# Three 256-column accumulations of a decoder layer's projections turned into 512-column ones with two halves

## The chip, the cores and the metric

One NeuronCore of a Trainium2 chip runs the whole layer. The metric is the device time of one execution in microseconds; lower is better. TensorE is called PE, VectorE DVE, ScalarE ACT, GpSimd POOL and SyncE SP, as in the profile.

## The reference, cut to what matters

A decoder layer of 256 tokens and width 1024: a SwiGLU half-step, a mixer with two groups of attention heads, cross-attention, a second SwiGLU half-step, and a final norm. The three projections of this case are the ones that add into the residual stream `x`:

```python
x = x + 0.5 * swiglu(rms_norm(x, g_ffn1), w_ffn1_gu, w_ffn1_down)   # down projection, 2816 -> 1024
h = rms_norm(x, g_mix)                                              # then h @ w_in, attention
...
x = x + concatenate([ya, yb]) @ w_out                               # output projection of the mixer
x = x + cross_attn(rms_norm(x, g_cross), rms_norm(mem, g_mem))      # ends with o @ w_co
x = x + 0.5 * swiglu(rms_norm(x, g_ffn2), w_ffn2_gu, w_ffn2_down)
```

Each of the three is followed by an RMS norm of the new `x` and a further projection of it (`w_in`, `w_cq`, `w_ffn2_gu`).

## The kernel before

**Number form.** A float32 operand is split into a high and a low part, and a product is high x high + low x high + high x low. Activations lie transposed, width on the partitions: a *slot* holds two contraction steps, each as 256 columns of the high part and 256 of the low part. Weights are loaded in tiles of 128 x 1024 (`raw`, four buffers), split by ACT (L125, high part) and DVE (L126, low part) into `w` (eight buffers), and the load of a tile goes out on SP's queue when its `raw` buffer is free again.

**Two ways to do one block.** A block is 128 of the 1024 output columns for all 256 tokens, accumulated in one PSUM bank. The first way (`mm2`, `mmT_run`) streams both halves of the slot in one matmul of 512 columns (L224) and the low weights against the high activations in one of 256 (L228): the bank ends with two halves that have to be added. The second way (`mm3`, L188 to L190) makes three matmuls of 256 columns into the same 256 columns of the bank.

**What follows a block.** `add_halves` adds the bank to the residual tile X0 to X7 (one per block). With 512 columns ACT copies the second half to `hv` (L301), DVE adds the first half to X (L302), then `hv` to X (L303). With 256 columns DVE does it in one instruction (L298). Then `block` makes the next projection's operand: ACT scales X into the high part of a slot (L323), DVE makes the low part (L324), ACT squares X into `sq` (L350), and POOL adds `sq` to the running sum `ssq` (L355). `hv` and `sq` share three buffers. When all eight are in, two statistics matmuls (L367, each of them two instructions for PE) sum `ssq` over the partitions; DVE (L328) and POOL (L330) make the norm's factor from it.

**The three places.** `downT` (L442) makes the down projection: two chunks of four blocks, 22 contraction steps; block 7 (the last of chunk 1) is done the second way. `addT` (L466) makes `w_out` and `w_co` with 8 steps; with `whole=c` the last block of chunk 1 is done the second way there too. For `w_co` the first chunk has an order of its own: the four blocks run side by side and end in the last round, one after the other. The next projection takes its steps in the order of X0 to X7, all four blocks abreast, so that X7 is needed last.

**What sets the order.** PE works in the order in which the program is written (`manual_schedule` for PE); small pieces of work that are put off by `later` come in when a running estimate of PE's time (`tick`) has passed their due time. The order on DVE, ACT, POOL and SP is set by the scheduler when the kernel is built, and each of these engines then works strictly in that order.

Of the kernel before, what the change touches and what calls it, by code (L numbers as in the profile page):

```python
# [21 lines left out]
FK = FF // P  # L22
# [6 lines left out]
def layer_kernel(ctx, tc, x_in, mem_in, g_ffn1, w_gu1, w_dn1, g_mix, w_in, rel_bias, g_out_a, g_out_b,  # L29
# [13 lines left out]
    def bank():  # L43
        return psp.tile([P, 512], F32, tag="bank", name="bank")
# [86 lines left out]
    def colchunk(wd, c0, n, nkt=KT):  # L131

        per = 1024 // n
        res = []
        for k0 in range(0, nkt, per):
            nk = min(per, nkt - k0)
            w = wload((lambda raw, nk=nk: raw[:, :nk * n].rearrange("p (a n) -> p a n", n=n),
                       cols(wd, k0, nk, c0, n), nk * n))
            res += [(w, i * n) for i in range(nk)]
        return res  # L140
# [36 lines left out]
    def tick(us):  # L177
        clock[0] += us
        pump()
# [7 lines left out]
    def mm3(ps, ah, al, bh, bl, start, stop):  # L187
        nc.tensor.matmul(ps, ah, bh, start=start, stop=False)  # L188
        nc.tensor.matmul(ps, al, bh, start=False, stop=False)  # L189
        nc.tensor.matmul(ps, ah, bl, start=False, stop=stop)  # L190
        tick(0.33 if ps.shape[-1] <= 256 else 0.65)

    def act(slots, k):

        s = slots[k // 2]
        o = (k % 2) * 512
        return s[:, o:o + 256], s[:, o + 256:o + 512]

    def both(slots, k):

        return slots[k // 2][:, (k % 2) * 512:(k % 2) * 512 + 512]

    def mm2(ps, wh, wl, xhl, start, stop):

        nc.tensor.matmul(ps, wh, xhl, start=start, stop=False)
        nc.tensor.matmul(ps[:, :256], wl, xhl[:, :256], start=False, stop=stop)
        tick(0.33)

    def mmT(ps, wk, xs, k, blk, start, stop):

        w, o = wk[k]
        o += blk * P
        if ps.shape[-1] == 512:
            mm2(ps, w[:, 0, o:o + P], w[:, 1, o:o + P], both(xs, k), start, stop)
        else:
            h, l = act(xs, k)
            mm3(ps, w[:, 0, o:o + P], w[:, 1, o:o + P], h, l, start, stop)

    def mmT_run(todo, wk, xs, first, last):


        for ps, k, blk in todo:
            w, o = wk[k]
            nc.tensor.matmul(ps, w[:, 0, o + blk * P:o + (blk + 1) * P], both(xs, k), start=k == first, stop=False)  # L224
            tick(0.23)
        for ps, k, blk in todo:
            w, o = wk[k]
            nc.tensor.matmul(ps[:, :256], w[:, 1, o + blk * P:o + (blk + 1) * P], both(xs, k)[:, :256],  # L228
                             start=False, stop=k == last)
            tick(0.12)  # L230

    def mmT_wide(pieces, wk, xs, k, start, stop):

        w, o = wk[k]
        h, l = act(xs, k)
        for i, (wp_, a) in enumerate(((0, h), (0, l), (1, h))):
            for blk, ps in enumerate(pieces):
                nc.tensor.matmul(ps, w[:, wp_, o + blk * P:o + (blk + 1) * P], a,  # L238
                                 start=start and i == 0, stop=stop and i == 2)
                tick(0.11)  # L240

    def projT(wk, xs, nblk, spread=False, whole=0, abreast=False):

        res = [bank() for _ in range(nblk)] if spread or abreast else []
        if spread and whole:
            res = [b[:, :256] for b in res]
            for k in range(KT):
                mmT_wide(res, wk, xs, k, k == 0, k == KT - 1)
            return res
        if spread:  # L250
            for k in range(KT):
                mmT_run([(res[blk], k, blk) for blk in range(nblk)], wk, xs, 0, KT - 1)
            return res
        if abreast:
            for b0 in range(0, nblk, 2):
                for k in range(0, KT, 2):
                    for blk in (b0, b0 + 1):
                        mmT_run([(res[blk], k, blk), (res[blk], k + 1, blk)], wk, xs, 0, KT - 1)
            return res
        return each(wk, xs, nblk, whole)  # L260

    def each(wk, xs, nblk, whole):
        for blk in range(nblk):
            b = bank()
            if blk >= nblk - whole:
                b = b[:, :256]
                for k in range(KT):
                    mmT(b, wk, xs, k, blk, k == 0, k == KT - 1)
            else:
                for k in range(0, KT, 2):  # L270
                    mmT_run([(b, k, blk), (b, k + 1, blk)], wk, xs, 0, KT - 1)
            yield b
# [23 lines left out]
    def add_halves(x, ps, scale):  # L296
        if ps.shape[-1] == 256:
            nc.vector.scalar_tensor_tensor(x, ps, scale, x, OP.mult, OP.add)  # L298
            return
        t = work.tile([P, 256], F32, tag="sq", name="hv", bufs=3)  # L300
        nc.scalar.activation(t, ps[:, 256:], AF.Copy, scale=scale)  # L301
        nc.vector.scalar_tensor_tensor(x, ps[:, :256], scale, x, OP.mult, OP.add)  # L302
        nc.vector.tensor_tensor(x, x, t, OP.add)  # L303
# [138 lines left out]
    def downT(w_dn, hid, block):  # L442

        for c in range(2):
            wk = colchunk(w_dn, c * 512, 512, FK)
            b = [bank() for _ in range(4)]
            if c == 1:
                b[3] = b[3][:, :256]

            def step(k, blk):  # L450
                if b[blk].shape[-1] == 512:
                    mmT_run([(b[blk], k, blk), (b[blk], k + 1, blk)], wk, hid, 0, FK - 1)
                else:
                    for i in (k, k + 1):
                        mmT(b[blk], wk, hid, i, blk, i == 0, i == FK - 1)

            for k in range(0, FK - 6, 2):
                for blk in range(4):
                    step(k, blk)
            for blk in range(4):  # L460
                for k in range(FK - 6, FK, 2):
                    step(k, blk)
                add_halves(X[c * 4 + blk], b[blk], 0.5)
                block(c * 4 + blk)

    def addT(wd, src, block, order=None):  # L466

        for c in range(2):
            wk = colchunk(wd, c * 512, 512)
            if c == 0 and order:  # L470
                b = [bank() for _ in range(4)]
                for step in order:
                    if callable(step):
                        step()
                        continue
                    k, blks = step
                    for blk in blks:
                        mmT_run([(b[blk], k, blk), (b[blk], k + 1, blk)], wk, src, 0, KT - 1)
                        if k == KT - 2:
                            add_halves(X[blk], b[blk], 1.0)  # L480
                            block(blk)
                continue
            for blk, ps in enumerate(projT(wk, src, 4, whole=c, abreast=(c == 0))):
                x = X[c * 4 + blk]
                add_halves(x, ps, 1.0)
                block(c * 4 + blk)
# [335 lines left out]
    with tc.manual_schedule(engines={mybir.EngineType.PE}):  # L822
        hid = gate_up(w_gu1, xs, st, (None, bias_table), (pg0, pu0))
        xs, st, block = next_x("mix")
        downT(w_dn1, hid, block)
        st.done()

# [4 lines left out]
        def head_pair(kt, op):  # L832
# [5 lines left out]
            elif kt == 7:  # L838
# [11 lines left out]
        until(lambda: len(ot) == 4)  # L850
        xs, st, block = next_x("cross")
        addT(w_out, ot, block)
        st.done(rows=False)
        PT = cross_qp(xs, K, st)
# [3 lines left out]
        xs, st, block = next_x("ffn2")  # L858
        every = range(4)
        addT(w_co, OT, block, ((0, every), (2, (0, 1)), lambda: cross_o(V, PT, OT, 2), (2, (2, 3)),  # L860
                               lambda: cross_o(V, PT, OT, 3), (4, every), (6, every)))
        st.done()

        hid = gate_up(w_gu2, xs, st, scale=0.5)
# [3 lines left out]
        ps = [[bank() for _ in HALVES] for _ in range(2)]  # L868
# [7 lines left out]
        def step(k, tb, w, p, c0, n):  # L876
            h, l = act(hid, k)
            t = slice(tb * P, tb * P + P)
            mm3(p, h[:, t], l[:, t], w[:, 0, c0:c0 + n], w[:, 1, c0:c0 + n], False, k == FK - 1)
# [78 lines left out]
```

## Time and profile before

| | us |
|---|---|
| median of 3 runs | 605.53 (605.5 to 606.17) |
| profiled execution | 605.74 |
| its span | 604.0 |
| PE busy | 595.4 |
| PE weight loads busy | 519.3 |
| DVE busy | 428.5 |
| ACT busy | 347.7 |
| POOL busy | 51.8 |

The profiled execution's time is 1.7 us above its span, which begins with the first and ends with the last instruction of the program. Busy times of PE overlap in the view, since a matmul's end is modelled; the distance from the start of one matmul to the start of the next tells what it costs. The mean granted clock of PE is 0.998 of full speed. On DVE and ACT as well the start of the next instruction can lie before the end of the last by some 0.1 us.

### The profile page before, as it was taken

How to read it: one execution, taken by the hardware profiler on the slowest of the kernel's cores; microseconds unless marked ns; L12 is line 12 of the kernel's file. 1: busy time of each engine (PE TensorE's matmuls, PEld its weight loads, DVE VectorE, ACT ScalarE, POOL GpSimd, SP SyncE). 2: the span in 40 equal slices, each digit the busy share in tenths (PEclk: the TensorE clock that was granted, in tenths of full speed). 3: DMA queues.
4: the chain of work that ended last, by engine and by line, in shares of the span. 5: the costliest groups of instructions: out<-in, count | busy, mean ns of one | idle time of the engine just before them, and what ended most of it. 6: DMA issues, size and time to landing. Idle time of an engine off the chain costs nothing.

```text
span 604.0 us, 9469 instructions
## 1 busy us (share of the span) xinstructions
PE 595.4 (99%) x3516; PEld 519.3 (86%) x3516; DVE 428.5 (71%) x716; ACT 347.7 (58%) x604; POOL 51.8 (9%) x83
## 2 busy tenths in 40 slices
PE   9999999999999999999999999999999999999995
PEld 8988888888899888888888899888888888888884
DVE  4788766887565876766897787869877877874412
ACT  6756446655554677656675565657755656653302
POOL 0000110000010102113300120003100000000000
PEclk9999999999999999999999999999999999999999
DMA  7867998677467636454446645444565565565401
GB/s 237 282 206 229 211 246 252 196 227 245 171 221 231 210 106 210 142 173 140 141 121 218 195 143 162 140 140 130 158 230 181 169 217 171 189 231 196 152 0 69
DMA packets 58989, 110.02 MB, mean 182 GB/s; under 512 B 3760, under 2 KB 14608, under 8 KB 58944
## 3 DMA queue, kind: packets, MB, share of 16 engines
q1 hardware_dynamic: 57664, 105.49, 54.1%
q0 software_dynamic: 832, 2.88, 2.8%
q10 hardware_dynamic: 448, 1.05, 0.5%
q8 instruction: 27, 0.44, 0.3%
q14 instruction: 18, 0.15, 0.1%
HBM read 107.58 MB, written 1.84 MB: 181 GB/s over the span
## 4 chain that ended last, share of the span: by engine, by line
PE 96%; issue 1%; DVE 1%; ACT 1%; POOL 0%; POOLq 0%; ACTq 0%
PE bank L224 43%; PE bank L228 22%; PE bank L188 7%; PE bank L189 7%; PE bank L190 7%; PE bank L238 5%; PE bank L518 1%; PE bank L575 1%; PE bank L558 1%; DVE w L126 0%; PE bank L770 0%; PE bank L382 0%; PE bank L779 0%; PE bank L873 0%; PE bank L604 0%
## 5 line engine op out<-in xcount | busy, mean ns | idle before, releaser
L224 PE MATMUL bank<-slot,w 128*128 128x512 f32 x1130 | 353.4, 396 | 0.0
L126 DVE TENSOR_TENSOR w<-raw,w 128x1024 fp32r<-128x1024 f32 (+1 forms) x197 | 237.3, 1219 | 84.5 <-ACT w L125 83.7
L125 ACT ACTIVATE w<-raw 128x1024 fp32r<-128x1024 f32 (+1 forms) x197 | 202.4, 1051 | 86.3 <-PE bank L190 43.4
L228 PEld LDWEIGHTS bank<-slot,w 128*128 128x128 f32 x1130 | 209.8, 188 | 48.7 <-issue 1.0
L228 PE MATMUL bank<-slot,w 128*128 128x256 f32 x1130 | 222.5, 279 | 0.0
L224 PEld LDWEIGHTS bank<-slot,w 128*128 128x128 f32 x1130 | 173.8, 189 | 2.5 <-issue 0.6
L188 PE MATMUL bank<-w,slot 128*128 128x512 f32 x152 | 60.0, 395 | 0.0
L190 PE MATMUL bank<-w,slot 128*128 128x512 f32 x152 | 59.3, 390 | 0.0
L189 PE MATMUL bank<-w,slot 128*128 128x512 f32 x152 | 59.2, 390 | 0.0
L277 ACT ACTIVATE hv<-bank 128x256 f32<-128x256 f32 x108 | 39.8, 375 | 33.7 <-PE bank L228 33.0
L320 ACT ACTIVATE slot<-u 128x512 fp32r<-128x512 f32 x22 | 13.8, 628 | 36.0 <-DVE u L434 36.0
L190 PEld LDWEIGHTS bank<-w,slot 128*128 128x128 f32 x152 | 28.5, 188 | 6.1
L188 PEld LDWEIGHTS bank<-w,slot 128*128 128x128 f32 x152 | 28.5, 188 | 6.0 <-issue 0.3
L189 PEld LDWEIGHTS bank<-w,slot 128*128 128x128 f32 x152 | 28.6, 188 | 5.5
L238 PE MATMUL bank<-slot,w 128*128 128x256 f32 x240 | 31.8, 290 | 0.0
L238 PEld LDWEIGHTS bank<-slot,w 128*128 128x128 f32 x240 | 30.1, 195 | 0.5 <-DVE slot L324 0.2
L355 POOL TENSOR_TENSOR ssq<-ssq,sq 128x256 f32<-128x256 f32 x22 | 20.5, 933 | 78.5 <-ACT sq L350 78.4
L429 ACT ACTIVATE g<-g 128x512 f32<-128x512 f32 x22 | 13.8, 631 | 20.1 <-DVE g L292 20.1
L324 DVE SCALAR_TENSOR_TENSOR slot<-X,gT,slot 128x256 fp32r<-128x256 f32 x30 | 19.4, 659 | 6.9 <-ACT slot L323 6.9
L321 DVE TENSOR_TENSOR slot<-u,slot 128x512 fp32r<-128x512 f32 x22 | 15.2, 691 | 10.7 <-ACT slot L320 10.5
L278 DVE TENSOR_TENSOR g<-bank,hv 128x256 f32<-128x256 f32 x40 | 16.5, 420 | 8.5 <-ACT hv L277 8.5
L323 ACT ACTIVATE slot<-X,gT 128x256 fp32r<-128x256 f32 x30 | 14.8, 506 | 13.0 <-DVE X L303 13.0
(128 smaller groups left out, 488.4 us busy)
## 6 DMA issues: line engine op xcount, KB each, us to landing
raw<-in_w_ffn_gu_dram SPq DMA_DIRECT2D x88, 512.0 KB, 4.6
raw<-in_w_ffn_down_dram SPq DMA_DIRECT2D x44, 512.0 KB, 4.3
raw<-in_w_ckv_dram SPq DMA_DIRECT2D x16, 512.0 KB, 5.5
raw<-in_w_in_dram SPq DMA_DIRECT2D x12, 512.0 KB, 3.7
raw<-in_w_in_dram SPq DMA_DIRECT2D x24, 256.0 KB, 4.0
raw<-in_w_out_dram SPq DMA_DIRECT2D x8, 512.0 KB, 4.5
raw<-in_w_cq_dram SPq DMA_DIRECT2D x8, 512.0 KB, 4.8
raw<-in_w_co_dram SPq DMA_DIRECT2D x8, 512.0 KB, 3.7
```

What stands on the lines that cost most here:

```text
L125: nc.scalar.activation(w[:, 0, a:b], raw[:, a:b], AF.Copy)
L126: nc.vector.tensor_tensor(w[:, 1, a:b], raw[:, a:b], w[:, 0, a:b].bitcast(F32), OP.subtract)
L188: nc.tensor.matmul(ps, ah, bh, start=start, stop=False)
L189: nc.tensor.matmul(ps, al, bh, start=False, stop=False)
L190: nc.tensor.matmul(ps, ah, bl, start=False, stop=stop)
L224: nc.tensor.matmul(ps, w[:, 0, o + blk * P:o + (blk + 1) * P], both(xs, k), start=k == first, stop=False)
L228: nc.tensor.matmul(ps[:, :256], w[:, 1, o + blk * P:o + (blk + 1) * P], both(xs, k)[:, :256], start=False, stop=k == last)
L238: nc.tensor.matmul(ps, w[:, wp_, o + blk * P:o + (blk + 1) * P], a, start=start and i == 0, stop=stop and i == 2)
L277: nc.scalar.activation(t, ps[:, 256:], AF.Copy)
L278: nc.vector.tensor_tensor(out, ps[:, :256], t, OP.add)
L324: nc.vector.scalar_tensor_tensor(l, src, g, h.bitcast(F32), OP.mult, OP.subtract)
L355: (eng or nc.gpsimd).tensor_tensor(new, self.ss, sq, OP.add)
```

## The change

The special case of the last block goes: in `downT` block 7 is accumulated in 512 columns by `mmT_run` like the other seven, and in `addT` the argument `whole=c` goes, with the same effect for block 7 of `w_out` and of `w_co`. Since `add_halves` looks at the width, these three blocks now take its three-instruction path.

```diff
         for c in range(2):
             wk = colchunk(w_dn, c * 512, 512, FK)
             b = [bank() for _ in range(4)]
-            if c == 1:
-                b[3] = b[3][:, :256]
 
             def step(k, blk):
-                if b[blk].shape[-1] == 512:
-                    mmT_run([(b[blk], k, blk), (b[blk], k + 1, blk)], wk, hid, 0, FK - 1)
-                else:
-                    for i in (k, k + 1):
-                        mmT(b[blk], wk, hid, i, blk, i == 0, i == FK - 1)
+                mmT_run([(b[blk], k, blk), (b[blk], k + 1, blk)], wk, hid, 0, FK - 1)
...
-            for blk, ps in enumerate(projT(wk, src, 4, whole=c, abreast=(c == 0))):
+            for blk, ps in enumerate(projT(wk, src, 4, abreast=(c == 0))):
                 x = X[c * 4 + blk]
                 add_halves(x, ps, 1.0)
                 block(c * 4 + blk)
```

PE's order is otherwise the same: 38 contraction steps have two matmuls instead of three, and everything else stands in its old order, the statistics matmuls too. POOL's and SP's orders are the same. On DVE and ACT the order changes at the three places only. The largest rearrangement is at the end of `w_co`. There `w_4674` to `w_4689` of the kernel before are the tiles of the first "up" chunk of the second SwiGLU, `w_4809`, `w_4814`, ... those of its next "gate" chunk; in the changed kernel the same tiles are called `w_4645` to `w_4660` and `w_4780`, `w_4785`, ... `slot_4273` (before) and `slot_4249` (now) hold X6 and X7.

DVE at the end of `w_co`, before, from the addition of X6 on:

```order
L302 SCALAR_TENSOR_TENSOR X6_94<-bank_4514,X6_94 128x256
L324 SCALAR_TENSOR_TENSOR slot_4273<-X7_95,gT_81,slot_4273 128x256
L303 TENSOR_TENSOR X6_94<-X6_94,hv_4531 128x256
L126 TENSOR_TENSOR w_4684<-raw_4682,w_4684 128x1024
L126 TENSOR_TENSOR w_4689<-raw_4687,w_4689 128x1024
L324 SCALAR_TENSOR_TENSOR slot_4273<-X6_94,gT_81,slot_4273 128x256
L126 TENSOR_TENSOR w_4809<-raw_4807,w_4809 128x1024
L126 TENSOR_TENSOR w_4814<-raw_4812,w_4814 128x1024
L328 TENSOR_SCALAR ms_4654<-bank_4651 128x2
```

DVE at the same place now:

```order
L126 TENSOR_TENSOR w_4660<-raw_4658,w_4660 128x1024
L303 TENSOR_TENSOR X6_94<-X6_94,hv_4507 128x256
L126 TENSOR_TENSOR w_4780<-raw_4778,w_4780 128x1024
L126 TENSOR_TENSOR w_4785<-raw_4783,w_4785 128x1024
L324 SCALAR_TENSOR_TENSOR slot_4249<-X6_94,gT_81,slot_4249 128x256
L302 SCALAR_TENSOR_TENSOR X7_95<-bank_4517,X7_95 128x256
L303 TENSOR_TENSOR X7_95<-X7_95,hv_4534 128x256
L126 TENSOR_TENSOR w_4790<-raw_4788,w_4790 128x1024
L324 SCALAR_TENSOR_TENSOR slot_4249<-X7_95,gT_81,slot_4249 128x256
L328 TENSOR_SCALAR ms_4625<-bank_4622 128x2
```

X7's addition and slot, which stood ahead of X6's, stand behind them now, and the splits of `w_4780` and `w_4785` (`w_4809` and `w_4814` before) have moved ahead of X6's slot.

ACT at the end of `w_co`, before, from the scaling of X5 on:

```order
L323 ACTIVATE slot_4272<-X5_93,gT_81 128x256
L350 ACTIVATE sq_4510<-X5_93 128x256
L301 ACTIVATE hv_4531<-bank_4514 128x256
L323 ACTIVATE slot_4273<-X7_95,gT_81 128x256
L125 ACTIVATE w_4689<-raw_4687 128x1024
L125 ACTIVATE w_4809<-raw_4807 128x1024
L323 ACTIVATE slot_4273<-X6_94,gT_81 128x256
L350 ACTIVATE sq_4537<-X6_94 128x256
L350 ACTIVATE sq_4569<-X7_95 128x256
L125 ACTIVATE w_4814<-raw_4812 128x1024
```

ACT at the same place now:

```order
L323 ACTIVATE slot_4248<-X5_93,gT_81 128x256
L350 ACTIVATE sq_4486<-X5_93 128x256
L301 ACTIVATE hv_4507<-bank_4490 128x256
L125 ACTIVATE w_4780<-raw_4778 128x1024
L125 ACTIVATE w_4785<-raw_4783 128x1024
L323 ACTIVATE slot_4249<-X6_94,gT_81 128x256
L350 ACTIVATE sq_4513<-X6_94 128x256
L301 ACTIVATE hv_4534<-bank_4517 128x256
L125 ACTIVATE w_4790<-raw_4788 128x1024
L323 ACTIVATE slot_4249<-X7_95,gT_81 128x256
L350 ACTIVATE sq_4540<-X7_95 128x256
```

The split of `w_4785` stands ahead of X6's scaling now (before, its counterpart `w_4814` stood behind X7's square), and X7's copy, scaling and square come after X6's.

## Rows read from the trace of the kernel before

**Rows 1.** The page: busy time of the engines; the chain by engine.
```profile
PE 595.4 (99%) x3516; PEld 519.3 (86%) x3516; DVE 428.5 (71%) x716; ACT 347.7 (58%) x604; POOL 51.8 (9%) x83
...
PE 96%; issue 1%; DVE 1%; ACT 1%; POOL 0%; POOLq 0%; ACTq 0%
```

**Rows 2.** Timeline of PE, down projection: start, us, engine, line, operation, out<-in, shapes, count.
```profile
184.03 0.28 PE L188 MATMUL bank<-slot,w 128*128 128x256 f32 x1
...
184.74 0.63 PE L224 MATMUL bank<-slot,w 128*128 128x512 f32 x2
```

**Rows 3.** Timeline of PE: begin of block 6, block 7 and what follows, `w_co`.
```profile
406.30 0.63 PE L224 MATMUL bank<-slot,w 128*128 128x512 f32 x2
...
409.09 0.28 PE L188 MATMUL bank<-slot,w 128*128 128x256 f32 x1
...
411.97 1.09 PE L224 MATMUL bank<-slot,w 128*128 128x512 f32 x4
```

**Rows 4.** Timeline of PE: steps of X6 and X7 in the projection behind `w_co`.
```profile
420.50 1.21 PE L224 MATMUL bank<-slot,w 128*128 128x512 f32 x4
421.55 0.40 PE L228 MATMUL bank<-slot,w 128*128 128x256 f32 x2
421.79 0.50 PE L367 MATMUL bank<-ones,ssq 128*128 128x2 f32 x4
...
422.47 1.08 PE L224 MATMUL bank<-slot,w 128*128 128x512 f32 x4
```

**Rows 5.** Timeline of ACT behind `w_co`; in brackets the idle time before and its releaser.
```profile
414.97 0.37 ACT L301 ACTIVATE hv<-bank 128x256 f32<-128x256 f32 x1
415.23 0.50 ACT L323 ACTIVATE slot<-X,gT 128x256 fp32r<-128x256 f32 x1
415.63 1.99 ACT L125 ACTIVATE w<-raw 128x1024 fp32r<-128x1024 f32 x2
...
419.03 1.07 ACT L125 ACTIVATE w<-raw 128x1024 fp32r<-128x1024 f32 x1 [0.39 <-DMA raw<-in_w_ffn_gu_dram]
```

**Rows 6.** Timeline of DVE behind `w_co`.
```profile
413.13 0.41 DVE L302 SCALAR_TENSOR_TENSOR X<-bank,X 128x256 f32<-128x256 f32 x1
413.46 0.41 DVE L298 SCALAR_TENSOR_TENSOR X<-bank,X 128x256 f32<-128x256 f32 x1
...
416.48 0.47 DVE L324 SCALAR_TENSOR_TENSOR slot<-X,gT,slot 128x256 fp32r<-128x256 f32 x1
416.88 0.41 DVE L303 TENSOR_TENSOR X<-X,hv 128x256 f32<-128x256 f32 x1
417.21 2.35 DVE L126 TENSOR_TENSOR w<-raw,w 128x1024 fp32r<-128x1024 f32 x2
419.48 0.96 DVE L324 SCALAR_TENSOR_TENSOR slot<-X,gT,slot 128x256 fp32r<-128x256 f32 x1
420.36 2.89 DVE L126 TENSOR_TENSOR w<-raw,w 128x1024 fp32r<-128x1024 f32 x2
```

**Rows 7.** Timeline of POOL behind `w_co`.
```profile
415.20 0.74 POOL L355 TENSOR_TENSOR ssq<-ssq,sq 128x256 f32<-128x256 f32 x1 [2.28 <-ACT sq L350]
418.47 2.56 POOL L355 TENSOR_TENSOR ssq<-ssq,sq 128x256 f32<-128x256 f32 x2 [2.53 <-ACT sq L350]
```

**Rows 8.** Instructions that write or read the tile raw, 403 to 425 us.
```profile
DMA to landing us min/median/max: 3.5/3.6/3.6
```

**Rows 9.** Timeline of PE and DVE behind the down projection and behind `w_out`.
```profile
199.30 0.96 DVE L324 SCALAR_TENSOR_TENSOR slot<-X,gT,slot 128x256 fp32r<-128x256 f32 x1
...
205.54 0.50 PE L367 MATMUL bank<-ones,ssq 128*128 128x2 f32 x4
...
206.22 1.08 PE L224 MATMUL bank<-slot,w 128*128 128x512 f32 x4
...
354.18 1.21 DVE L126 TENSOR_TENSOR w<-raw,w 128x1024 fp32r<-128x1024 f32 x1
...
362.46 0.50 PE L367 MATMUL bank<-ones,ssq 128*128 128x2 f32 x4
```

**Rows 10.** Busy time by stretch: us, PE, PEld, DVE, ACT, POOL, PEclk, DMA, GB/s.
```profile
380.00:390.00 10.00, 9.36 (x66) 8.43 (x65) 9.25 (x18) 7.25 (x15) 0.00 (x0) 1.00 0.59 167
```

## The prediction

> **What bounds the kernel now.** I read the page first: TensorE (PE) is busy for 595.4 of 604.0 us and 96% of the chain that ended last is PE's [rows 1]. So two things count: how long PE's own stream is, and where PE has to wait. The change shortens the stream a little and lengthens, at three places, what VectorE (DVE) and ScalarE (ACT) do after the last block. I therefore went to PE's timeline at the three places for the price of a block, and then to the places where PE first needs what the last block leaves behind. There are two such needs: the slot of X7 (the eighth contraction step of the next projection), and the sum of squares, which the statistics matmuls (L367) read. The statistics matmuls stand in the middle of the seventh step at the third place: two of four L228, then L367 at 421.79, then the other two [rows 4]. PE works in its written order, so whoever makes L367 late makes everything behind it late.
>
> **What PE saves.** A pair of contraction steps was six matmuls of 256 columns; it becomes two of 512 and two of 256, the same 1536 columns. In w_co's last-but-one block (that form already) four pairs take 409.09 - 406.30 = 2.79 us; the last block takes 411.97 - 409.09 = 2.88 [rows 3]. So 0.09 us at each output projection. In the down projection a pair of the old form takes 0.71 us [rows 2] against 2.79 / 4 = 0.70; over 11 pairs that is 0.1 to 0.25, and I take 0.2. Together 0.3 to 0.45, taken as 0.4 us, all of it on the path. [...]
>
> **What is added.** Each last block had one DVE instruction (L298, 0.41 us) from PSUM into X. Now it has an ACT copy of the second half (L301, 0.37 [rows 5]), a DVE multiply-add (L302) and a DVE add (L303), each 0.41 like L298 [rows 6]. Three times 1.2 us on engines with room: by busy time it costs nothing. It costs where PE is waiting at the end of the chain. So I go through the places.
>
> **First place, the down projection.** The next projection needs X7's slot after seven of its eight steps, at 206.22, and the statistics at 205.54 [rows 9]. X7's slot was ready at 199.30 + 0.96 = 200.3. Two short instructions and the two or three weight splits that the new order puts ahead of it (1.14 us each, from 417.21 to 419.48 for two [rows 6]) make it some 203. Covered by about 3 us: nothing.
>
> **Second place, w_out.** Here the ACT queue decides. The new order has X6, then a copy for X7, then two weight splits, then X7. The second of these needs a load that is issued only when an earlier split has freed its buffer. In the old order a split at 354.18 frees one [rows 9]; in the new one the split moves up by the two instructions that no longer stand ahead of it, 0.66 us, to 353.52, and ends at 354.7. A load lands 3.6 us after issue [rows 8], 358.4; ACT's split takes 1.07 [rows 5], then X7's scaling and square 0.8: 360.2. POOL adds the square by 361.1 if free, 361.9 if DVE holds it up as in [rows 7]. L367 starts at 362.46 [rows 9]. That is 0.5 us or more of cover: nothing, but little.
>
> **Third place, w_co.** Here there is no cover. The order of w_co ends its first four blocks together, so ACT and DVE are behind: block 6 leaves PE at 409.09, but its copy runs at 414.97 [rows 3, 5]. PE already waited a little for X6's slot in the kernel before: ready at 419.48 + 0.96 = 420.44, and PE's step starts at 420.50 [rows 4, 6]. X7 was ahead of X6 then, since its short form jumped the queue (L298 at 413.46, slot at 416.48). In the changed order X7 comes last, and more weight splits stand before X6. I walk the new DVE order with the start-to-start times of [rows 6] (0.33 for L302, L303; 1.14 for a split; 0.88 for L324 with POOL beside it, 0.40 alone):
> X5's L302 at 413.13, unchanged; split 413.46; X5's L303 414.60; split 414.93; X5's slot 416.07; X6's L302 416.95; split 417.28; X6's L303 418.41; two splits 418.74 and 419.88; X6's slot at 421.0, ready at 421.5 to 422.0; X7's L302 421.4 to 421.9, its L303 done 422.1 to 422.6. The second of those two splits follows ACT's, and ACT's waits for a load issued at the end of the split of 413.46, at 414.7: landed 418.3, split by 419.4. So DVE is the later of the two, and the load, in front of X6 in ACT's queue, is hidden by 0.5 us.
> Then ACT: X7's scaling 0.40 and square 0.40 to 423.0 or 423.5. POOL's add takes 0.1 to start and 0.74 [rows 7], up to 1.0 with a split beside it: 423.9 to 424.6. PE's L367 follows 0.1 us behind, at 424.0 to 424.7 instead of 421.79. **Lost: 2.2 to 2.9 us**; I take 2.5, since POOL and DVE do overlap in this walk. In it lies the earlier wait for X6's slot, 421.5 or later instead of 420.50. X7's slot, after one more split, comes at 423.7 to 424.6 and is needed 0.68 us behind L367 (422.47 - 421.79), so it adds nothing.
> The spread between the ends comes from POOL and DVE: L324 takes 0.47 alone (416.48) and 0.96 while POOL adds (419.48), and POOL's two adds took 2.56 instead of 1.48 [rows 6, 7]. [...]
>
> **Sum.** The 0.3 us gained at the first two places moves the start of this chain forward with PE; the 0.09 of the third block doesn't, as PE waits anyway. 2.5 - 0.3 = 2.2 us (1.9 to 2.6). Behind this stretch PE's stream is gapless and gives nothing back. Against the profiled execution, 605.74: 607.9. The median of the runs, 605.53, lies 0.2 below it: **607.7 to 607.8**. What a measurement can tell from no change is about 0.2%, 1.2 us: above 606.7 counts as slower.
>
> **Rivals.** (a) *Not slower.* The last block's chain stays under PE's work at the third place as at the other two, and only the gain is left: 605.5 - 0.4 = 605.1. It decides at two points: X6's slot ready by 420.4 and the squares summed by 421.7. For it speaks that the other two places have 3 and 0.5 us of cover by the same rows; against it that the walk misses these points by 1.1 and 2.2 us, and that X6's slot was already late. It would need two of the splits to be out of the way. Chance 0.13. (b) *A second hole, at w_out.* If the load behind ACT's split takes 1 us longer, or POOL is held up twice, L367 at 362.46 slips by up to 0.7, on top of the forecast: 608.3 to 608.6. Chance 0.07. (c) *The clock falls in the new holes.* Two waits of about 1 us each within 4 us are new. Were the granted clock halved for the next 2.5 to 5 us of work, that work would take twice as long: 610.3 to 612.8. Against it: around 384 PE had about 0.6 us without work and the granted clock stayed 1.00 [rows 10]. Chance 0.03. (d) *Faster by over 1.2 us*: the saved PE time has 0.45 us at most, and no row shows a wait that the change takes away. Chance 0.01. That the change does nothing is excluded: PE's order has 38 matmuls fewer.
>
> **How the numbers follow.** The forecast has 0.76, from 607.3 to 608.4. With (b) it gives slower 0.83 and (c) brings 0.86; since the walk has some twenty steps, I move 0.02 of it to "same". The range takes the forecast's ends, 0.4 us for the load and POOL on either side, and most of (b): 606.9 to 608.9, leaving out (a), (c) and (d). A single case, a missed cover of 2.5 us, carries the verdict.
>
> **What would show it.** In the profile of the changed kernel: block 7 of each projection 0.70 us per pair; no idle PE before L367 at the first and second place; at the third, PE waiting for DVE's L324 of X6 some 1.1 us and then at L367 for POOL some 1.1 us, with L367 about 12.4 us behind the end of block 7 rather than 9.8. The chain that ended last would pass there through DVE's weight splits and POOL. I am wrong if PE stays gapless there (then 605.1), or if a wait shows elsewhere.

## The result and the profile after

The changed kernel takes **610.99 us** (median of 8 executions, 607.71 to 613.85) against 605.53 (605.14 to 606.63): ratio 1.0083, 95% interval 1.0057 to 1.0109. It is slower, by 5.5 us where 2.2 were forecast. The profiled execution is the fastest of the eight, 607.71 us, with a span of 605.9 and a mean granted clock of 0.998. The others spread, and their clock goes with their time:

| execution | us | mean granted clock of PE |
|---|---|---|
| profiled | 607.71 | 0.998 |
| | 608.25 | 0.998 |
| | 610.58 | 0.995 |
| | 610.83, 611.14, 611.34, 611.96 | 0.993 |
| | 613.85 | 0.990 |

The kernel before showed 0.998 in its profiled execution and 0.996 to 0.999 in all that ran beside the experiments below. So the profile after shows the kernel as it was forecast, and the table shows that most executions had something else besides. First the profile.

The page: PE is busy for 0.7 us less than in [rows 1], DVE 1.8 and ACT 1.4 us more, and of the chain that ended last PE has 93% instead of 96%, DVE 2% instead of 1%, and a DMA 1%.

```profile
PE 594.7 (98%) x3478; PEld 516.5 (85%) x3478; DVE 430.3 (71%) x719; ACT 349.1 (58%) x607; POOL 52.2 (9%) x83
...
PE 93%; DVE 2%; DMA 1%; issue 1%; ACT 1%; POOL 0%; SPq 0%; POOLq 0%; ACTq 0%; DVEq 0%
```

The timeline of PE at the third place (start, us, engine, line, operation; in brackets the idle time before and what ended it), which answers to [rows 3, 4]:

```profile
408.12 0.63 PE L224 MATMUL bank<-slot,w 128*128 128x512 f32 x2
...
410.90 0.86 PE L224 MATMUL bank<-slot,w 128*128 128x512 f32 x3
...
418.85 0.64 PE L228 MATMUL bank<-slot,w 128*128 128x256 f32 x4
421.03 1.19 PE L224 MATMUL bank<-slot,w 128*128 128x512 f32 x4 [1.55 <-DVE slot L324]
422.07 0.39 PE L228 MATMUL bank<-slot,w 128*128 128x256 f32 x2
423.64 0.61 PE L367 MATMUL bank<-ones,ssq 128*128 128x2 f32 x4 [1.18 <-POOL ssq L355]
424.11 0.48 PE L228 MATMUL bank<-slot,w 128*128 128x256 f32 x2
...
428.62 0.61 PE L382 MATMUL bank<-dg,ones 128*128 128x128 f32 x4
```

Block 7 runs from 408.12 to 410.90, 2.78 us. Then come the two holes: PE waits for X6's slot (DVE) and then, in the middle of that step, for the sum of squares (POOL). L367 stands 12.74 us behind the end of block 7 instead of 9.82. L382, a later step of the same norm, follows 4.98 us behind L367.

The timeline of DVE there, from X5's L302 on, answers to [rows 6]:

```profile
412.14 0.41 DVE L302 SCALAR_TENSOR_TENSOR X<-bank,X 128x256 f32<-128x256 f32 x1
...
417.76 2.35 DVE L126 TENSOR_TENSOR w<-raw,w 128x1024 fp32r<-128x1024 f32 x2
420.03 0.95 DVE L324 SCALAR_TENSOR_TENSOR slot<-X,gT,slot 128x256 fp32r<-128x256 f32 x1
420.90 0.41 DVE L302 SCALAR_TENSOR_TENSOR X<-bank,X 128x256 f32<-128x256 f32 x1
421.35 0.42 DVE L303 TENSOR_TENSOR X<-X,hv 128x256 f32<-128x256 f32 x1
421.78 1.23 DVE L126 TENSOR_TENSOR w<-raw,w 128x1024 fp32r<-128x1024 f32 x1
422.92 0.94 DVE L324 SCALAR_TENSOR_TENSOR slot<-X,gT,slot 128x256 fp32r<-128x256 f32 x1
```

DVE has no gap from one row to the next: X6's slot (420.03) waits for nothing but the two weight splits ahead of it. ACT and POOL there, [rows 5, 7]:

```profile
417.22 1.06 ACT L125 ACTIVATE w<-raw 128x1024 fp32r<-128x1024 f32 x1 [1.13 <-DMA raw<-in_w_ffn_gu_dram]
...
421.81 0.51 ACT L323 ACTIVATE slot<-X,gT 128x256 fp32r<-128x256 f32 x1 [1.13 <-DVE X L303]
422.22 0.40 ACT L350 ACTIVATE sq<-X 128x256 f32<-128x256 f32 x1
```

```profile
419.13 1.57 POOL L355 TENSOR_TENSOR ssq<-ssq,sq 128x256 f32<-128x256 f32 x1 [3.37 <-ACT sq L350]
422.76 0.82 POOL L355 TENSOR_TENSOR ssq<-ssq,sq 128x256 f32<-128x256 f32 x1 [2.07 <-ACT sq L350]
```

The chain into L367 reads: X6's slot done at 420.98, X7 added by 421.77, scaled and squared by 422.62, summed by POOL at 423.58, L367 at 423.64.

At the other two places [rows 9] PE's timeline has no idle time ahead of L367. At `w_out`, however, ACT waits for a load right up to the point where the cover ends:

```profile
204.57 0.50 PE L367 MATMUL bank<-ones,ssq 128*128 128x2 f32 x4
...
361.41 0.58 PE L367 MATMUL bank<-ones,ssq 128*128 128x2 f32 x4
```

```profile
358.42 1.06 ACT L125 ACTIVATE w<-raw 128x1024 fp32r<-128x1024 f32 x1 [2.04 <-DMA raw<-in_w_co_dram]
```

### The profile page after: what moved, and what is told of

Same layout as the page of the kernel before. It is cut to its first block, busy times and chain, and to the rows that moved or that the text cites. A ratio compares the mean times of both kernels' runs of the same rounds, so it can differ in the third digit from the quotient of the medians.

```text
span 605.9 us, 9403 instructions
## 1 busy us (share of the span) xinstructions
PE 594.7 (98%) x3478; PEld 516.5 (85%) x3478; DVE 430.3 (71%) x719; ACT 349.1 (58%) x607; POOL 52.2 (9%) x83
## 4 chain that ended last, share of the span: by engine, by line
PE 93%; DVE 2%; DMA 1%; issue 1%; ACT 1%; POOL 0%; SPq 0%; POOLq 0%; ACTq 0%; DVEq 0%
PE bank L224 43%; PE bank L228 22%; PE bank L188 6%; PE bank L189 6%; PE bank L190 6%; PE bank L238 4%; DMA raw<-in_w_ffn_gu_dram 1%; PE bank L512 1%; DVE w L126 1%; PE bank L569 1%; PE bank L552 1%; ACT w L125 1%; PE bank L382 0%; PE bank L367 0%; DVE slot L324 0%
## 5 line engine op out<-in xcount | busy, mean ns | idle before, releaser
L224 PE MATMUL bank<-slot,w 128*128 128x512 f32 x1168 | 365.3, 396 | 1.6 <-DVE slot L324 1.6
L228 PEld LDWEIGHTS bank<-slot,w 128*128 128x128 f32 x1168 | 216.9, 188 | 50.4 <-issue 1.0
L228 PE MATMUL bank<-slot,w 128*128 128x256 f32 x1168 | 229.9, 279 | 0.0
L224 PEld LDWEIGHTS bank<-slot,w 128*128 128x128 f32 x1168 | 179.6, 189 | 4.1 <-DVE slot L324 1.8
L238 PE MATMUL bank<-slot,w 128*128 128x256 f32 x240 | 31.5, 287 | 0.1
L238 PEld LDWEIGHTS bank<-slot,w 128*128 128x128 f32 x240 | 29.5, 191 | 0.8 <-DVE slot L324 0.4
L324 DVE SCALAR_TENSOR_TENSOR slot<-X,gT,slot 128x256 fp32r<-128x256 f32 x30 | 20.0, 674 | 6.9 <-ACT slot L323 6.9
L278 DVE TENSOR_TENSOR u<-bank,hv 128x256 f32<-128x256 f32 x40 | 16.8, 419 | 8.4 <-ACT hv L277 8.2
```

The lines of the kernel that those rows point to most:

```text
L278: nc.vector.tensor_tensor(out, ps[:, :256], t, OP.add)
L324: nc.vector.scalar_tensor_tensor(l, src, g, h.bitcast(F32), OP.mult, OP.subtract)
```

## The experiments

Two theories were open after the result. **H1**: all of the loss comes from the two holes at `w_co`, of which the second part is not in the profile: behind the holes the granted clock falls in most executions. **H2**: the loss beyond the forecast comes from elsewhere, from `w_out` or from the longer path on DVE and ACT as such. In what follows "a low clock" is a mean granted clock of an execution of 0.995 or less, which the kernel before never showed.

### The changed kernel again: where the other executions lose time

Three more profiles of the unchanged `after` kernel: `again` (timed too), `again2` and `again3`.

> The changed kernel once more, to see its spread and where its slower executions lose time. Theory A (the granted clock falls behind the two new holes in most executions): times of 607.5 to 608.3 go with a mean granted clock of 0.998 and times of 610 to 614 with 0.990 to 0.995, and a trace of a longer execution shows the clock at half somewhere between 420 and 430 us, with the holes as long as in the first trace (1.7 and 1.3 us). Theory B (the holes themselves vary, since the load or POOL in front of them varies): a longer execution has a hole that is 3 to 5 us longer, and the clock is 1.0 there.

> The changed kernel once more, for a profile of another execution. If a mean granted clock of 0.993 is two stretches of 3.4 us at half clock, an execution with that mean shows two such stretches and some 3.4 us more than the execution of 607.71; with 0.995 one stretch and 1.7 us.

> The same as the run before it: one more execution of the changed kernel with its profile, to see how many stretches at half clock stand in it and where.

Measured: `again` 611.08 us (609.8 to 612.13), ratio 1.0089 (1.0075 to 1.0104), all six executions with a low clock; its profiled one took 609.84 us at 0.995. The profile of `again2` took 612.55 us at 0.994, that of `again3` 611.15 at 0.993. The busy time by stretch of `again` (columns as in [rows 10]; the eighth value is the granted clock):

```profile
415.00:424.90 9.90, 7.17 (x42) 6.01 (x41) 9.45 (x13) 5.69 (x11) 2.89 (x3) 1.00 0.84 259
424.90:428.30 3.40, 3.40 (x12) 2.92 (x12) 1.21 (x5) 1.03 (x4) 0.70 (x1) 0.50 0.54 181
428.40:435.00 6.60, 6.60 (x41) 5.84 (x40) 4.34 (x9) 4.32 (x7) 0.00 (x0) 1.00 0.26 81
```

The same view of `again3`:

```profile
415.00:423.60 8.60, 6.43 (x36) 5.25 (x34) 8.52 (x12) 5.50 (x11) 1.94 (x3) 1.00 0.87 266
423.70:430.40 6.70, 6.13 (x20) 5.37 (x21) 3.08 (x8) 2.15 (x5) 1.22 (x2) 0.50 0.39 126
430.50:440.00 9.50, 9.50 (x58) 8.35 (x57) 5.88 (x11) 4.94 (x8) 0.00 (x0) 1.00 0.19 57
```

And PE's timeline of `again3` through the second hole:

```profile
421.66 1.21 PE L224 MATMUL bank<-slot,w 128*128 128x512 f32 x4 [1.68 <-DVE slot L324]
422.71 0.40 PE L228 MATMUL bank<-slot,w 128*128 128x256 f32 x2
424.27 1.01 PE L367 MATMUL bank<-ones,ssq 128*128 128x2 f32 x4 [1.15 <-POOL ssq L355]
...
425.71 1.91 PE L224 MATMUL bank<-slot,w 128*128 128x512 f32 x4
...
432.06 0.60 PE L382 MATMUL bank<-dg,ones 128*128 128x128 f32 x4
```

The holes are those of the first profile. Behind them the granted clock is 0.50 of full speed: four matmuls of 512 columns take 1.91 us (`again3`, 425.71) instead of 1.09 [rows 3]. In `again` this lasts 3.4 us (424.9 to 428.3), in `again3` 6.8 us (423.6 to 430.4), in `again2` 6.8 us as well (425.3 to 432.2): one stretch of twice the length, not two apart as was expected of `again2`. What a stretch costs is read from L367 to L382, between which PE has the same work in all four profiles and no wait: 4.98 us in the first profile, 6.53 in `again` (424.21 to 430.74), 8.08 in `again2` (425.37 to 433.45) and 7.79 in `again3`. So a stretch of 3.4 us loses 1.55 us, and one of 6.8 us loses 3.1, or 2.8 where its first 0.66 us fall into the hole itself (`again3`, 423.61 to 424.27).

This adds up to the measured times with one thing that the change has no part in. How far PE is with its work near the start of the program varies from execution to execution: four matmuls there begin at 7.77 us in the first profile of the changed kernel, at 8.35 in `again3` and at 9.00 in `again2`. The same four in the timeline of PE before and after:

```profile
8.59 0.60 PE L779 MATMUL bank<-ident,slot 128*128 128x128 f32 x4
```

```profile
7.77 0.60 PE L773 MATMUL bank<-ident,slot 128*128 128x128 f32 x4
```

The profile after starts 0.8 us earlier than the one before, which is luck. In `again2` L367 at `w_co` stands 1.73 us later than in the first profile of the changed kernel (1.09 of it are there at L367 of the first place already, 205.66 against 204.57, and 0.43 are added up to L367 at `w_out`, where PE has a wait of 0.27): 607.71 + 1.73 + 3.1 = 612.5, measured 612.55. For `again3`: 607.71 + 0.63 + 2.8 = 611.1, measured 611.15. For `again`: 607.71 + 0.57 + 1.55 = 609.8, measured 609.84.

### Which place does it: the parts of the change alone

The down projection alone, `addT` as before; from the kernel before:

```diff
-            if c == 1:
-                b[3] = b[3][:, :256]
...
```

> Only the down projection changed. The run with down projection and w_out changed was bimodal (7 of 12 executions at 605.1 to 605.7, 5 at 606.9 to 609.2), and its trace has a wait of 1.0 us at the statistics matmuls behind w_out. Theory: that wait belongs to w_out alone. Then this kernel has no wait at 362 us, no execution above 606.7, and a median of 605.2 to 605.4, 0.2 us below the kernel before. Rival: the down projection's shift brings it about; then it is bimodal as well.

Measured: 605.39 us (604.93 to 606.02, 11 executions), ratio 0.9998 (0.9989 to 1.0006), no low clock. The first place costs nothing, and the 0.2 us gained there are too small to be told from nothing.

The down projection and `w_out`, with `w_co` as before; from the changed kernel:

```diff
-    def addT(wd, src, block, order=None):
+    def addT(wd, src, block, order=None, whole=0):
...
-            for blk, ps in enumerate(projT(wk, src, 4, abreast=(c == 0))):
+            for blk, ps in enumerate(projT(wk, src, 4, whole=c * whole, abreast=(c == 0))):
...
-                               lambda: cross_o(V, PT, OT, 3), (4, every), (6, every)))
+                               lambda: cross_o(V, PT, OT, 3), (4, every), (6, every)), whole=1)
```

> Only the down projection and w_out changed; the last block of w_co stays in 256 columns with its one-instruction addition. If the third place alone makes the loss (both theories): 605.1 to 605.3, that is 0.3 us below the kernel before, no new hole, mean clock 0.998 in every execution. If the other two places cost as well, more than 605.6.

Measured: 605.63 us (605.06 to 609.15, 12 executions), ratio 1.0014 (0.9999 to 1.003). The executions fall into two groups: seven from 605.06 to 605.67, and five at 606.93, 608.11, 608.3, 608.57 and 609.15, of which the last four have a low clock (0.994 or 0.995). The profiled one is that of 606.93. Its PE and its ACT at `w_out`, and the load issued at 354.9:

```profile
363.56 0.61 PE L367 MATMUL bank<-ones,ssq 128*128 128x2 f32 x4 [0.84 <-POOL ssq L355]
```

```profile
360.60 1.06 ACT L125 ACTIVATE w<-raw 128x1024 fp32r<-128x1024 f32 x1 [3.24 <-DMA raw<-in_w_co_dram]
```

```profile
DMA to landing us min/median/max: 5.6/5.6/5.6
```

So the second place has a hole too, in a part of the executions: the load lands 5.6 us after its issue, ACT's split starts at 360.60, and everything behind it in ACT's queue, X7's scaling and square, is late. In the first profile of the changed kernel the same load took 4.5 us, and the cover just sufficed. What was expected if the third place alone makes the loss, no new hole and a clock of 0.998 in every execution, did not come. At `w_co` this profile has no wait ahead of L367 (422.97). So the low clock of the other four executions is hard to put down to holes at `w_co`. The profiled one's 606.93 and the 1.55 us of a short stretch make 608.5, which lies among their 608.11 to 609.15: a fall behind the hole at `w_out` is the likely reading, but none of the four has a profile, so it is not shown.

`w_co` alone, the other two as before; from the kernel before:

```diff
-    def addT(wd, src, block, order=None):
+    def addT(wd, src, block, order=None, whole=1):
...
-            for blk, ps in enumerate(projT(wk, src, 4, whole=c, abreast=(c == 0))):
+            for blk, ps in enumerate(projT(wk, src, 4, whole=c * whole, abreast=(c == 0))):
...
-                               lambda: cross_o(V, PT, OT, 3), (4, every), (6, every)))
+                               lambda: cross_o(V, PT, OT, 3), (4, every), (6, every)), whole=0)
```

> Only the last block of w_co changed. If the third place alone makes the loss: 607.7 where the clock stays and 610 to 614 where it falls, a median near 611, 0.3 us above the fully changed kernel. If the three places add up, less than half of the loss.

Measured: 609.81 us (608.29 to 611.77, 4 executions), ratio 1.0072 (1.005 to 1.0094): 608.29 and 608.63 at 0.998 and 0.997, 610.98 and 611.77 at 0.993. Its profile (608.29) has the two holes, of 1.55 and 1.08 us. `w_co` alone brings the two holes and a low clock, and most of the loss; with two falls in four executions the median, expected near 611, says little more. H2's "elsewhere" is `w_out`: it leaves the median of `co_old` where it was, but makes five of its twelve executions 1.7 to 3.9 us longer than the median of the other seven (605.26).

### Is it the holes: PE kept busy in them

In the changed kernel PE gets matmuls of 256 columns whose result nobody reads, 13 ahead of X6's step and 10 ahead of L367; the orders of the other engines are the same.

```diff
+                if fillers and k == 6:
+                    d = bank()
+                    def keep_busy(n):
+                        w, o = wk[6]
+                        for _ in range(n):
+                            nc.tensor.matmul(d[:, :256], w[:, 0, o:o + P], both(xs, 5)[:, :256], start=True, stop=True)
+                    fillers.append(keep_busy)
+                    keep_busy(fillers[0])
...
+            if len(fillers) == 3:
+                fillers.pop()(fillers[1])
...
+        fillers.extend((13, 10))
```

> The changed kernel with 13 matmuls of 256 columns ahead of X6's step and 10 ahead of the statistics matmuls, on data that is there (their result is not used), so that TensorE works through nearly all of both holes (1.56 of 1.7 us and 1.2 of 1.3) and the wait for DVE and POOL stays as long. Theory A: the clock stays, mean 0.998 in every execution, and all times lie at 607.4 to 608.0. Theory B: the times still spread from 607.5 to 614, median near 611.

Measured: 609.13 us (608.83 to 610.21, 6 executions), ratio 1.0061 (1.0049 to 1.0073), clocks 0.997 to 0.999. PE's timeline (L258 are the fillers, L381 is L367):

```profile
420.77 0.64 PE L228 MATMUL bank<-slot,w 128*128 128x256 f32 x4
421.24 1.72 PE L258 MATMUL bank<-slot,w 128*128 128x256 f32 x13
422.97 1.19 PE L224 MATMUL bank<-slot,w 128*128 128x512 f32 x4
424.00 0.40 PE L228 MATMUL bank<-slot,w 128*128 128x256 f32 x2
424.24 1.35 PE L258 MATMUL bank<-slot,w 128*128 128x256 f32 x10
425.59 0.61 PE L381 MATMUL bank<-ones,ssq 128*128 128x2 f32 x4
```

PE has as little useful to do as before, but is not idle there (busy for 7.99 of the 8.00 us from 418 to 426), and no execution has a low clock. The waits themselves stay: L381 stands 12.77 us behind the end of block 7 (412.82 to 425.59). The times were expected at 607.4 to 608.0 and came out 1 to 2 us above that. For the profiled execution (609.72, 2.0 us above the first profile of the changed kernel) the trace shows why: PE begins its work behind `w_out` 0.55 us later (351.54 against 350.99), and at the statistics matmuls there it is 1.90 us later (363.31 against 361.41). The 1.35 us between are lost behind a load that landed after 5.9 us; 0.82 of them are a wait ahead of L381. The other five have no profile.

Then one hole each: fillers in the first only (`fill_first`, 13 and 0), and in the second only (`fill_second`, 0 and 10).

> The changed kernel with TensorE kept busy in the first hole only (13 matmuls ahead of X6's step). If the sum of both holes makes the clock fall: hardly any fall, 608 to 609, mean clock 0.997 or more. If the second hole is enough by itself: falls as in the changed kernel, 610 to 612, mean clock 0.993 to 0.995.

> The changed kernel with TensorE kept busy in the second hole only (10 matmuls ahead of the statistics matmuls). If the sum of both holes makes the clock fall: hardly any fall, 608 to 609. If the first hole, the longer one, is enough: falls as in the changed kernel, 610 to 612, mean clock 0.993 to 0.995.

The edit of `fill_first` against `fill_both`, and of each profile the hole that is left (`fill_first`, then `fill_second`):

```diff
-        fillers.extend((13, 10))
+        fillers.extend((13, 0))
```

```profile
423.95 0.61 PE L381 MATMUL bank<-ones,ssq 128*128 128x2 f32 x4 [1.15 <-POOL ssq L367]
```

```profile
421.24 1.19 PE L224 MATMUL bank<-slot,w 128*128 128x512 f32 x4 [1.55 <-DVE slot L336]
```

Measured: `fill_first` 608.29 us (607.98 to 612.15, 6 executions), ratio 1.0055 (1.0036 to 1.0075), one low clock (612.15 at 0.994); `fill_second` 609.45 us (607.94 to 610.1, 5 executions), ratio 1.0063 (1.005 to 1.0077), no low clock. With one of the two holes filled the clock fell in 1 of 11 executions, with both open in 14 of the 16 of the changed kernel. The changed kernel did not run beside these two, but `early` below did, and there the clock falls. Whether the one fall of `fill_first` came behind the hole at `w_co` or behind one at `w_out` is not shown. `fill_second`'s three executions from 609.45 to 610.1 have a clock of 0.998 or 0.999; no profile shows them, and what they lost is open (a late load at `w_out` as in `fill_both` would be of the size).

### The hole without the change

The kernel before, with the statistics matmuls written 2.4 us earlier, so that PE meets one long wait for the same sum:

```diff
-        st.done()
+        st.done(delay=7.1)
```

> The kernel before, with the statistics matmuls behind w_co put 2.4 us earlier in TensorE's order, so that TensorE waits there once for POOL's last sum (ready at 421.0, asked for at some 419.3): one hole of 1.7 us, nothing else changed up to there. If holes cost their length alone: 607.1 to 607.3, mean clock 0.998. If a single hole of this length makes the clock fall: part of the executions 1.7 us higher still, 608.8 to 609.

Measured: 608.62 us (606.97 to 609.09, 5 executions), ratio 1.0043 (1.003 to 1.0055): 606.97 and 607.2 at 0.997 and 0.999, the other three 608.62 to 609.09 at 0.994 to 0.996. PE's timeline and the stretches of the profiled one (608.62):

```profile
418.60 0.40 PE L224 MATMUL bank<-slot,w 128*128 128x512 f32 x1
420.68 0.61 PE L367 MATMUL bank<-ones,ssq 128*128 128x2 f32 x4 [1.69 <-POOL ssq L355]
```

```profile
415.00:421.50 6.50, 4.81 (x30) 4.01 (x29) 6.50 (x8) 4.31 (x7) 3.02 (x3) 1.00 0.56 181
421.60:425.00 3.40, 3.40 (x13) 2.81 (x12) 2.41 (x6) 1.06 (x1) 1.61 (x1) 0.50 0.81 257
```

One hole of 1.69 us, in a kernel that has nothing of the change, is followed by a stretch of 3.4 us at half clock. That cost 1.55 us in `again`, and the two groups here lie 1.4 to 2.1 us apart. So the fall belongs to the hole and not to the 512-column block.

### The change with cover

If the holes are all, independent work in them must give the whole loss back. The down projection and `w_co` as in the change, `w_out` as before, and in the second SwiGLU's first chunk two "up" blocks are drawn forward:

```diff
+            elif c == 0 and cover:
+                wg, wu = colchunk(w_gu, 0, n), colchunk(w_gu, FF, n)
+                pg = [bank() for _ in range(4)]
+                pu = [bank() for _ in range(2)]
+                for ks in (range(0, 6), range(6, KT)):
+                    for k in ks:
+                        mmT_run([(pg[blk], k, blk) for blk in range(4)], wg, xs, 0, KT - 1)
+                    for blk in range(2):
+                        for k in range(ks[0], ks[-1] + 1, 2):
+                            mmT_run([(pu[blk], k, blk), (pu[blk], k + 1, blk)], wu, xs, 0, KT - 1)
...
-        st.done()
+        st.done(delay=13.5)
...
+        hid = gate_up(w_gu2, xs, st, scale=0.5, cover=True)
```

> The down projection and w_co in halves as in the changed kernel, w_out as before; behind w_co the second SwiGLU's first chunk is written in another order: its gate blocks with X0 to X5, then two of its up blocks with X0 to X5 (4.2 us of work that needs neither X6 nor X7), then both with X6 and X7; the statistics matmuls stand 4 us later. If all that is lost at w_co is the two waits (for X6's slot and for the statistics) and the clock that falls in them, there is no wait over 0.3 us between 416 and 430, the granted clock is 0.996 or more in every execution, and the time is that of the kernel before less the 0.3 us of matmuls: 605.0 to 605.5. If the longer path behind X6 and X7 costs by something else (the splits that follow it on DVE, the norm's row that the gate blocks wait for), the time stays at 606.5 or more.

Measured: **605.01 us** (604.6 to 606.05, 11 executions) against 605.43 (605.18 to 605.88), ratio 0.9995 (0.9985 to 1.0004), clocks 0.997 to 0.999. PE and DVE of its profile:

```profile
419.83 0.63 PE L224 MATMUL bank<-slot,w 128*128 128x512 f32 x2
...
424.01 1.09 PE L224 MATMUL bank<-slot,w 128*128 128x512 f32 x4
424.94 0.50 PE L367 MATMUL bank<-ones,ssq 128*128 128x2 f32 x4
```

```profile
420.54 0.97 DVE L324 SCALAR_TENSOR_TENSOR slot<-X,gT,slot 128x256 fp32r<-128x256 f32 x1
...
423.35 0.96 DVE L324 SCALAR_TENSOR_TENSOR slot<-X,gT,slot 128x256 fp32r<-128x256 f32 x1
```

DVE does X6's and X7's slots as late as in the changed kernel (0.5 us later on the axis, as PE is), but PE has the drawn-forward work from 419.83 to 424.01, X6's step then starts on a slot that was ready at 421.51, and L367 follows without a wait. The whole loss at `w_co` is gone; `w_out` is as in the kernel before, so this run says nothing of the second place. The median is 0.4 us below the kernel before, about what PE's shorter stream should bring, but the interval holds 1: it is no measurable gain.

## Why the prediction was right and where it was wrong

**PE's saving: right in size.** Block 7 of `w_co` takes 2.78 us (2.79 forecast). Up to the end of block 7 the profile after is 1.07 us ahead of [rows 3] (410.90 against 411.97), of which 0.78 are there before the first of the three places (L98 starts at 59.23 instead of 60.01). So some 0.3 us were gained in three projections where 0.4 was taken.

**First place: right.** X7's slot is done at 201.96; the profile after runs 0.97 us ahead there (L367 at 204.57 against 205.54 in [rows 9]), so that is 202.9 where "some 203" was forecast, and no wait of PE follows. `dn_only` shows that no execution loses there.

**Second place: the mis-sized term is the load.** The forecast let it land 3.6 us after issue, by [rows 8] from another place, and found 0.5 us of cover. The new order issues the loads there 1.5 us apart (353.8 and 355.3 in the profile after) where they were 3.0 apart, and the load took 4.5 us, in other profiles of this order 4.4 to 5.9; with the old order it took 3.6 to 3.9. The cover is gone at about 4.7, an estimate from `co_old`, where 5.6 makes a hole of 0.84 us. Rival (b) had that mechanism with a landing "1 us longer" and a chance of 0.07; in `co_old` it comes in five of twelve executions, and with a fall of the clock behind it, if that is what the four are, it costs more than the 0.7 us of the rival. It doesn't decide the verdict. That the closer issue is the cause fits all profiles at this place, but was not tested by itself, and elsewhere the distance to the next load does not settle the landing: in the kernel before a load issued at 381.3, 1.5 us ahead of the next, landed after 3.5 us.

**Third place: the mechanism right, at the upper end.** The walk's points in its own frame (profile after plus 0.99 us, by X5's L302 at 412.14 against 413.13): X6's slot ready at 421.97 (forecast 421.5 to 422.0), POOL's sum at 424.57 (423.9 to 424.6), L367 at 424.63 (424.0 to 424.7). Lost: 2.84 us of the 2.2 to 2.9, against 2.5 taken. ACT's early split for the load was hidden as forecast: done at 418.28, ahead of the second of DVE's two splits at 418.9. The upper end holds because POOL and DVE do meet. POOL's add starts at 419.13 during a weight split and takes 1.57, and X6's L324, which starts behind it, takes 0.95 against 0.47 with no add beside it [rows 6]. The 0.74 of [rows 7] is an add that started at 415.20 just ahead of DVE's L324 (415.27), and there DVE's took 0.96. Elsewhere in the kernel before, L324 took 0.97 us where the add had begun ahead of it (412.24, the add at 411.92) and 0.49 where the add began 0.35 us behind its start (407.06, the add at 407.41). Why the two lengthen each other is not shown.

**The forecast of 607.8** is met by the executions without a fall of the clock, 607.71 and 608.25. The first is closer than it deserves: some 0.3 us too little for the holes is set off by a start that came 0.8 us earlier.

**What failed: the clock behind the holes, left to rival (c).** The sum prices the new holes by their length alone. That PE would work at half clock behind them stands only in rival (c), and I gave it 0.03. The step that failed is its evidence against: "around 384 PE had about 0.6 us without work and the granted clock stayed 1.00" [rows 10]. That row speaks of idle time of 0.6 us; the forecast itself had two holes of 1.1 us each, and they came out as 1.55 and 1.18. A row for a smaller hole bounds nothing for larger ones, and no row read from the kernel before has a hole of this size in the middle of the program.

What the runs show in its place:

- two holes in a row at `w_co`: low clock in 14 of 16 executions and, in `co_new`, in 2 of 4;
- the second alone, 1 of 6; the first alone, 0 of 5;
- one of 1.69 us in the old kernel: 3 of 5 executions 1.4 to 2.1 us longer than the other two;
- no new hole (`dn_only` and `cover`), 0 of 22; both holes filled (`fill_both`), 0 of 6;
- no hole at `w_co`, but one at `w_out` in a part of the executions (`co_old`): 4 of 12.

The lost work of (c), 2.5 to 5 us, was taken from no row: the stretches lose 1.55 us or 2.8 to 3.1. Its times, 610.3 to 612.8 us, hold 11 of the 16 executions of the changed kernel: 607.8 and the 2.8 to 3.1 us of a long stretch lie inside them, and nine executions have the clock of a long one (0.993 or 0.994). So of the 5.5 us, some 2.5 are the holes less the gain (2.84 - 0.3), and the rest is for the most part PE at half clock behind them, by execution 1.55 or 2.8 to 3.1 us; a late load at `w_out` comes on top in some (0.43 us in `again2`). Whether one execution shows a short stretch, a long one or none is not settled by anything seen here. Nor is the one execution at 0.990 (613.85); a fall at `w_out` besides the long stretch at `w_co` would come near it, but has no profile.

## What to carry to other kernels

A shorter stream on the busiest engine is worth nothing where it makes the last step of a chain longer than the work that covers it: some 0.3 us were saved here, and a sum of squares that came 2.8 us later cost nine times that, and the clock behind it up to as much again (1.55 to 3.1 us). Before such a change, write down for each place how many microseconds of independent work stand between a result and its first reader; where there is none, draw some forward first, as `cover` does. And price a new hole on PE not only by its length: look for the longest hole in the old trace behind which the granted clock stayed up (here some 0.6 us), and where the new one is longer (here 1.55 and 1.18), give a fall of the clock a real chance and a price from the stretch that a fall lasts (here 3.4 or 6.8 us).

## What was unexpected in the hardware

- A stretch at half clock lasted 3.4 us in two profiles (`again`, `early`) and 6.8 us in two (`again2`, `again3`), and in all four it began inside the last hole or up to 0.9 us behind it, then went back to full clock while PE worked on without a gap. PE was at work for all of it but 0.66 us in `again3`, with 1.71 us instead of 0.93 from four matmuls of 512 columns to the next step.
- Filling one of two holes with matmuls that do nothing made the kernel faster in the median (`fill_first` 608.29 against 611.08 of the same kernel without them), although the fillers leave the waits as long as they were; what they save is the clock, which is low in one of six executions against six of six.
- The same load of 512 KB behind `w_out` landed after 3.6 to 3.9 us in the order in which the next one was issued 3 us later, and after 4.4 to 5.9 us in the order in which the next one followed after 1.5 us. In the second order it varies by 1.5 us from execution to execution, with nothing changed ahead of it.
- The same four matmuls near the start (L773) begin at 7.77, 8.35 and 9.00 us in three profiles of the changed kernel (the first one, `again3` and `again2`), and the first and the last of them reach L367 of the first place 1.1 us apart (204.57 and 205.66), which is more than all that the change was to save.
